# A convolution branch loaded into another tile and closed behind four projections, and the last attention head closed one pair later

## The chip, the cores and the metric

The kernel runs on one core of a Trainium2 chip. A core has five engines that run at the same time, each through its own queue of instructions in a fixed order: TensorE (PE in the profile) multiplies matrices, its weight loads are shown apart as PEld; VectorE (DVE) and ScalarE (ACT) work elementwise; GpSimd (POOL) does small elementwise work and issues DMAs; SyncE (SP) issues DMAs. An engine whose next instruction waits for a semaphore holds everything behind that instruction. The metric is the device time of one execution in microseconds (us). The kernel before took 1056.47, 1059.1 and 1056.67 us in three runs, median 1056.67.

## The reference

One layer of a streaming encoder on 512 tokens of width 1024, in float32. Four mixers are fed from one normed input and one combined projection, then gated, merged and projected:

```python
h = _rms_norm(x, norm_mix_pre[l])
(a_q, a_k, a_v, f_q, f_k, f_v, f_g, c_u, s_x, s_b, s_c) = jnp.split(h @ w_in[l], cuts, axis=-1)
ya = _diff_attention(...)                  # A: 4 heads, two score maps each, then an RMS norm per head
yf = _forgetting_attention(...)            # F: 8 heads, a cumulative log-forget bias
c_a, c_g = jnp.split(c_u + b_glu[l], 2, axis=-1)
yc = _dwconv_causal(c_a * jax.nn.sigmoid(c_g), conv_dw[l]) + conv_dw_b[l]
yc = jax.nn.silu(_layer_norm(yc, conv_ln_g[l], conv_ln_b[l]))      # C: convolution branch
ys = s_b * _dwconv_causal(s_c * s_x, sc_w[l])                      # D: short convolution
br = jnp.stack([ya, yf, yc, ys], axis=2)
proj = jnp.einsum('bsnc,ncd->bsnd', br, w_branch[l])
gates = jax.nn.sigmoid(h @ w_gate[l] + b_gate[l]).reshape(B, S, N_BRANCH, D)
mixed = jnp.sum(gates * proj, axis=2) @ w_out[l]
```

Behind the mixers come a cross-attention into 256 memory tokens and a gated MLP of width 2816. They are computed by code that the change leaves alone.

## The kernel before

Every product is made three times from split operands: a float32 value is held as a high part (a cast) and a low part (the value less its high part), and `mm3` multiplies high by high, high by low and low by high. A weight block of 128x1024 is loaded by SP into one of two `wr` tiles, cast by ACT into `wh` (line 190), and DVE makes `wl` (line 191); both have four buffers. A projection to 128 channels is 24 matmuls of 128x512 into one PSUM bank. In the stretch that matters here all projections take turns in the two banks with the tag `mm`: a projection can start only when the one two before it has been read out of its bank.

`run_blocks` walks a list of such jobs, fetches weights three jobs ahead, and after each job lets background generators (`bg`) put some of their steps into the program: the depthwise convolution and its norm (`conv_task`, `conv_norm_task`), the attention heads (`a_task`, `f_task`). A generator's `yield` says how much work the step was and how long it should wait. So the order in which instructions are written comes from this interleaving. The tile framework then sets each engine's final order with a simulated timeline; `tc.issue_after(x)` keeps an instruction behind instruction x. Tiles come from pools in rings: with `bufs=2` the third allocation of a tag takes the first one's place and waits for its last reader.

The order of jobs in the stretch: values of the A heads; queries and keys of head 0; of head 1; two gate blocks of branch C; queries and keys of head 2; four blocks of C; head 3; six blocks of C; values of the F heads; queries and keys of F pair 0; of pair 1; blocks of branch A's gate; and so on to pair 3.

What the change and the prediction touch:

- `conv_norm_task`. The convolution's result is turned to token-major through DRAM into the tile `xn`, normed, turned back through DRAM (`conv_chan`, line 720) and loaded into `xn` again by four POOL DMAs (line 724). For each of four channel blocks j, ACT then makes an Identity and a Tanh of it (lines 737, 738), DVE joins them (line 739), and `split` writes the high part on ACT (line 158) and the low part on DVE (line 159) into `y["c"]`. Blocks 0 and 1 come as soon as they can; blocks 2 and 3 wait for the keys of head 0. `xn` is in the ring `qk` with two buffers, which also holds the queries and keys of each head, so head 1's `qk` tile is `xn`'s.
- `qk_jobs`. `body_q` clears two parts of the `qk` tile on POOL (line 804) and reads the bank in two halves: ACT copies one half (line 808), DVE takes its low part (line 809), then the same for the other. `body_k` does so with two ACT copies each (lines 816, 817) and a low part (line 818). After `body_k` the dictionary `key_ends` holds the last two instructions.
- `a_task`. A head's four query tiles of 128 make scores (PE, bank tag `sc`), a masked maximum (DVE, line 882), Exp (ACT, line 887), a scaling (ACT, line 891, and DVE, line 892), transposes (PE, line 236) and products with the values. At its end the head's output goes twice through DRAM (`turn`), and line 917 on ACT scales it into the tile `z`; `split` writes it into `y["a"]`. The output tile `o` is in the ring `ck`, `z` in the ring `fbias`.
- `f_task`. The F pairs use the rings `ck` (rows of the forget bias) and `fbias` (bias tiles), and the ring `e` of three buffers that all heads use for their softmax. Pair 0 starts behind pair 1's keys.
- `mixer_jobs`. Head 3 (name `a3` in the background) is run to its end before the jobs of F pair 0.

Of the kernel before, what the change touches and what calls it, by code (L numbers as in the profile page):

```python
# [25 lines left out]
P = 128  # L26
# [57 lines left out]
def hybrid_layer(ctx: ExitStack, tc: tile.TileContext, a: dict, out: bass.AP):  # L84
# [228 lines left out]
    def e4(dtype=F32):  # L313
        return m1p.tile([P, 2, S], dtype, tag="e", name="e", bufs=3)
# [266 lines left out]
    def y8(dtype=F32R):  # L581
        return m2p.tile([P, 4, S], dtype, tag="y8", name="y8", bufs=2)

    def y8b():
        return m2bp.tile([P, 4, S], F32R, tag="y8b", name="y8b", bufs=2)

    acc = [m2p.tile([P, S], F32, tag=f"acc{m}", name=f"acc{m}") for m in range(NK)]
    y = {}
# [63 lines left out]
        yield 0.5, 0.0  # L652

    conv_ends = []
    key_ends = {}

    def conv_task(j):
        n = 31
# [29 lines left out]
        yield 0.0, 5.0  # L688

    def conv_norm_task():  # L690
        xn = m1p.tile([P, 5, S], F32, tag="qk", name="xn", bufs=2)
        tok, chan = (dram.tile([P, NT * S], F32, name=n) for n in ("conv_tok", "conv_chan"))
        yield 0.0, 2.0
        while len(conv_ends) < 4:
# [24 lines left out]
            yield 0.65, 0.0  # L719
        G.dma_start(chan, conv_y.rearrange("p j c -> p (j c)"))  # L720
        yield 0.0, 4.0
        form = chan.rearrange("(b r) (a x) -> a r b x", r=32, a=4)
        for a_ in range(4):
            G.dma_start(xn[a_ * 32:a_ * 32 + 32, :4], form[a_])
        yield 0.0, 5.0
        turned_y = xn[:, :4].rearrange("p b (j t c) -> p j t b c", j=4, t=NT)
        while "d" in y:
            yield 0.0, 2.0
        yield 0.0, 2.0
        y["c"] = (y8(), y8())  # L730
        for j in range(4):
            while j > 1 and (O_AK, 0) not in key_ends:
                yield 0.0, 0.5
            e = e4()
            one, two = (e[:, i].rearrange("p (t b c) -> p t b c", t=NT, b=4) for i in range(2))
            with tc.issue_after(key_ends[O_AK, 0][0]) if j > 1 else ExitStack():
                A.activation(one, turned_y[:, j], AF.Identity, bias=pc("ln_b", j), scale=pc("ln_g", j))
                A.activation(two, turned_y[:, j], AF.Tanh, bias=half["ln_b"][:, j:j + 1], scale=half["ln_g"][:, j:j + 1])
# [56 lines left out]
    def qk_jobs(cq, ck, j, then, tag=None):  # L795


        st = {}
        rows = (slice(0, HD), slice(HD, P))

        def body_q(hi, lo):
            qk = st["qk"] = m1p.tile([P, 6, S], F32R, tag="qk", name="qk", bufs=2)
            for c, r in enumerate(rows):
                G.memset(qk[rows[1 - c], 4 + c].bitcast(F32), 0.0)
            ps = bank(tag)
            channel_major(ps, (hi, lo), ht)
            for c, r in enumerate(rows):
                A.copy(qk[r, c], ps[r])
                V.tensor_tensor(qk[rows[1 - c], c], ps[r], qk[r, c].bitcast(F32), ALU.subtract)

        def body_k(hi, lo):
            qk = st["qk"]
            ps = bank(tag)
            channel_major(ps, (hi, lo), ht)
            for c, r in enumerate(rows):
                A.copy(qk[r, 2 + c], ps[r])
                copy = A.copy(qk[rows[1 - c], 2 + c], ps[r])
                low = V.tensor_tensor(qk[r, 4 + c], ps[r], qk[r, 2 + c].bitcast(F32), ALU.subtract)
            key_ends[ck, j] = copy.ins, low.ins
# [35 lines left out]
    def head_tile(tag):  # L855
        return m1p.tile([P, S], F32, tag=tag, name=f"head_{tag}", bufs=2)
# [3 lines left out]
    def a_task(h, qk, v):  # L860
# [56 lines left out]
        A.activation(z.rearrange("p (t b c) -> p t b c", t=NT, b=4), o.rearrange("p (b t c) -> p t b c", b=4, t=NT),  # L917
                     AF.Identity, scale=half["dn"])
        split(z, y["a"][0][:, h], y["a"][1][:, h])
        yield 0.6, 0.0  # L920

# [88 lines left out]
    def f_task(p, qk, v):  # L1010
# [6 lines left out]
            G.dma_start(t, crows[2 * p + j:2 * p + j + 1, :].rearrange("a s -> (a s)").partition_broadcast(P))  # L1017
            ck.append(t)
        yield 0.0, 2.0
        while p == 0 and (O_FK, 1) not in key_ends:  # L1020
            yield 0.0, 0.5
        es, pts, av = {}, None, None
        for step in range(6):
# [17 lines left out]
            if step < 4:  # L1041
# [3 lines left out]
                for j in range(2):  # L1045
# [9 lines left out]
                    with tc.issue_after(key_ends[O_FK, 1][1]) if p + step == 0 else ExitStack():  # L1055
# [59 lines left out]
    def then(f):  # L1115

        return None, None, f
# [4 lines left out]
    def mixer_jobs():  # L1122
# [687 lines left out]
```

## Time and profile before

| what | value |
|---|---|
| median of 3 runs | 1056.67 us (1056.47 to 1059.1) |
| the profiled execution | 1056.2 us |
| its span, first to last instruction | 1054.4 us |
| PE busy in the span | 1041.7 us, 99% |
| PEld, DVE, ACT, POOL busy | 84%, 76%, 48%, 17% |
| mean granted TensorE clock | 0.996 |
| chain of work that ended last, on PE | 96% |

The profile is one execution. Rows of its timeline give the start of an instruction from the span's start, its duration, engine, line, operation and output<-input; in square brackets stands how long the engine had been idle before it and what ended that. "x4" means four such instructions in a row, put together. Matmuls are pipelined: a row's duration reaches over the start of the next, and the distance between the starts is what a matmul takes from PE's time. So a short wait of PE is hard to see as idle time, and is read from the starts.

### The profile page before, as it was taken

The page shows a single profiled execution, that of the slowest core. Times are in us where ns is not written, and L with a number is a line of the kernel's source. Part 1 is how long each engine was busy: PE and PEld are TensorE (multiplying, and loading weights), DVE is VectorE, ACT ScalarE, POOL GpSimd, SP SyncE. Part 2 cuts the span into 40 slices and gives each one's busy share as a digit, 9 for nine tenths or more (in the row PEclk, how much of TensorE's full clock was granted, in tenths as well). Part 3 has the DMA queues.
Part 4 walks back from the last instruction along what each step waited for, and adds up shares of the span by engine and source line. Part 5 has one row for each costly group of instructions (what it writes and reads, how often), then busy time and mean ns, then how long its engine had stood idle before and what let it go on. Part 6 is the DMA issues. An engine that isn't in the chain of part 4 may idle for free.

```text
span 1054.4 us, 14556 instructions
## 1 busy us (share of the span) xinstructions
PE 1041.7 (99%) x5295; PEld 886.0 (84%) x5295; DVE 806.4 (76%) x1280; ACT 501.4 (48%) x823; POOL 182.4 (17%) x309
## 2 busy tenths in 40 slices
PE   9999999999999999999999999999999999999996
PEld 8888888888888988888888899988888888888885
DVE  6999997677767477867487798777878777777795
ACT  5322222286565374655444566554333333355571
POOL 4000000200231233433011031121112111111001
PEclk9999999999999999999999999999999999999998
DMA  8954334742342353232358644236577676626662
GB/s 262 298 165 103 102 100 141 196 112 87 105 138 83 100 161 101 80 100 82 99 167 276 216 132 129 60 104 196 186 241 231 212 234 213 198 81 211 207 191 81
DMA packets 165373, 163.08 MB, mean 155 GB/s; under 512 B 6527, under 2 KB 136172, under 8 KB 165045
## 3 DMA queue, kind: packets, MB, share of 16 engines
q1 hardware_dynamic: 152995, 119.91, 38.0%
q0 software_dynamic: 5824, 19.03, 6.0%
q10 hardware_dynamic: 6482, 23.21, 5.8%
q8 instruction: 42, 0.69, 0.3%
q14 instruction: 30, 0.25, 0.1%
HBM read 139.03 MB, written 23.09 MB: 154 GB/s over the span
## 4 chain that ended last, share of the span: by engine, by line
PE 96%; DMA 1%; DVE 1%; ACT 1%; issue 1%; POOL 1%; POOLq 0%; DVEq 0%; SPq 0%; ACTq 0%
PE ps_mm L232 51%; PE ps_av L232 30%; PE ps_sc L232 8%; PE ps_tr L232 4%; PE ps_tr L236 2%; DMA wide<-in_w_out 1%; DMA xs<-in_x 0%; POOL st_r L271 0%; DVE nt L281 0%; POOL st_m L268 0%; ACT hth L432 0%; ACT wa L412 0%; ACT wh L190 0%; DVE wl L191 0%; POOL st_m L270 0%
## 5 line engine op out<-in xcount | busy, mean ns | idle before, releaser
L190 ACT CAST wh<-wr 128x1024 fp32r<-128x1024 f32 (+1 forms) x142 | 148.8, 1049 | 262.7 <-PE ps_mm L232 165.6
L191 DVE TENSOR_TENSOR wl<-wr,wh 128x1024 fp32r<-128x1024 f32 (+1 forms) x142 | 178.2, 1256 | 72.2 <-ACT wh L190 72.0
L232 PE MATMUL ps_mm<-hth,wh 128*128 128x512 f32 (+1 forms) x592 | 221.2, 380 | 0.3 <-ACT hth L155 0.2
L232 PE MATMUL ps_mm<-htl,wh 128*128 128x512 f32 (+1 forms) x592 | 220.5, 379 | 0.2 <-DVE htl L156 0.2
L232 PE MATMUL ps_mm<-hth,wl 128*128 128x512 f32 (+1 forms) x592 | 220.4, 379 | 0.0
L232 PE MATMUL ps_av<-htl,wh 128*128 128x512 f32 (+1 forms) x352 | 131.8, 374 | 0.0
L232 PE MATMUL ps_av<-hth,wh 128*128 128x512 f32 (+1 forms) x352 | 131.8, 374 | 0.0
L232 PE MATMUL ps_av<-hth,wl 128*128 128x512 f32 (+1 forms) x352 | 131.6, 374 | 0.0
L232 PEld LDWEIGHTS ps_mm<-hth,wh 128*128 128x128 f32 x592 | 109.7, 188 | 21.1 <-ACT hth L155 0.8
L232 PEld LDWEIGHTS ps_mm<-hth,wl 128*128 128x128 f32 x592 | 109.5, 188 | 20.2
L232 PEld LDWEIGHTS ps_mm<-htl,wh 128*128 128x128 f32 x592 | 109.5, 188 | 20.0 <-DVE htl L156 0.4
L665 DVE SCALAR_TENSOR_TENSOR y<-y,par,y 128x482 f32<-128x482 f32 (+29 forms) x120 | 83.3, 735 | 0.1
L232 PEld LDWEIGHTS ps_av<-hth,wl 128*128 128x128 f32 x352 | 66.2, 188 | 11.7
L232 PEld LDWEIGHTS ps_av<-htl,wh 128*128 128x128 f32 x352 | 66.1, 188 | 11.8
L232 PEld LDWEIGHTS ps_av<-hth,wh 128*128 128x128 f32 x352 | 66.1, 188 | 11.8
L1603 DVE TENSOR_TENSOR wl<-dw,wh 128x1024 fp32r<-128x1024 f32 x32 | 40.1, 1262 | 12.9 <-ACT wh L1602 12.7
L1602 ACT CAST wh<-dw 128x1024 fp32r<-128x1024 f32 x32 | 33.5, 1052 | 23.1 <-PE ps_mm L232 7.4
L1049 POOL TENSOR_SCALAR fbias<-ck,cq 128x128 f32<-128x128 f32 (+3 forms) x32 | 27.7, 872 | 63.6 <-DVE st L1056 57.2
L1551 ACT ACTIVATE th<-c 128x512 f32<-128x512 f32 x22 | 13.9, 632 | 47.7 <-DVE c L594 47.7
L155 ACT CAST pth<-ps_tr 128x512 fp32r<-128x512 f32 (+3 forms) x56 | 23.6, 449 | 26.2 <-PE ps_tr L236 25.9
L594 DVE SCALAR_TENSOR_TENSOR c<-ps_mm,par,c 128x510 f32<-128x510 f32 (+1 forms) x44 | 32.7, 744 | 0.7
L156 DVE TENSOR_TENSOR ptl<-ps_tr,pth 128x512 fp32r<-128x512 f32 (+3 forms) x56 | 27.5, 512 | 7.2 <-ACT pth L155 7.1
(491 smaller groups left out, 2130.6 us busy)
## 6 DMA issues: line engine op xcount, KB each, us to landing
wr<-in_w_up SPq DMA_DIRECT2D x44, 512.0 KB
wr<-in_w_in SPq DMA_DIRECT2D x38, 512.0 KB
wr<-in_w_gate SPq DMA_DIRECT2D x32, 512.0 KB
wp<-in_w_down ACTq DMA_DIRECT2D x22, 512.0 KB
sums<-wp ACTq DMA_DIRECT2D x22, 512.0 KB
dw<-sums SPq DMA_DIRECT2D x44, 256.0 KB
wr<-in_w_branch SPq DMA_DIRECT2D x16, 512.0 KB
wide<-in_w_out SPq DMA_DIRECT2D x12, 512.0 KB
```

Of the source, the lines that this page charges most:

```text
L155: A.copy(hi, ps)
L156: V.tensor_tensor(lo, ps, hi.bitcast(F32), ALU.subtract)
L190: order(A.copy(hi, raw[:, :n]))
L191: low.tensor_tensor(lo, raw[:, :n], hi.bitcast(F32), ALU.subtract)
L232: PE.matmul(ps, lhs, rhs, start=start, stop=stop)
L236: PE.transpose(ps, x, ident[:n, :n])
L594: ins = V.scalar_tensor_tensor(dst[:, s:], src[:, :S - s], w(k), dst[:, s:], ALU.mult, ALU.add)
L665: ins = V.scalar_tensor_tensor(dst[:, s:], src[:, :S - s], pc("conv_dw", k * 4 + j), dst[:, s:], ALU.mult, ALU.add)
L1049: G.tensor_scalar(bias[:, :w], ck[j][:, :w], -1.0, cq[:, qt, head:head + 1], ALU.mult, ALU.add)
L1551: A.activation(th, c[:, 0], AF.Tanh, scale=0.5)
L1602: A.copy(hi, x)
L1603: V.tensor_tensor(lo, x, hi.bitcast(F32), ALU.subtract)
```

## The change

The convolution branch's channel-major data no longer goes back into `xn`. It is loaded into a tile of the ring `y8b`, which holds the branch D operand before and the branch A operand later and is free in between; the load waits in the program until the D operand is dropped. `xn` itself stays in the ring `qk` for the token-major part only. Its four channel blocks are put behind four projections in turn: block 0 behind head 0's queries, 1 behind its keys, 2 behind head 1's queries, 3 behind its keys. `qk_ends` takes the place of `key_ends` and records queries too.

For head 3 the output tile and `z` are the two halves of one tile of the ring `e`, where they were in `ck` and `fbias`. The head is run up to the issue of its last DMAs before F pair 0's jobs; the closing activation and the split come behind the keys of F pair 1, and F pair 0 starts behind them.

```diff
-    def y8b():
-        return m2bp.tile([P, 4, S], F32R, tag="y8b", name="y8b", bufs=2)
+    def y8b(dtype=F32R):
+        return m2bp.tile([P, 4, S], dtype, tag="y8b", name="y8b", bufs=2)
...
     def conv_norm_task():
-        xn = m1p.tile([P, 5, S], F32, tag="qk", name="xn", bufs=2)
+        xn = m1p.tile([P, 6, S], F32, tag="qk", name="xn", bufs=2)
...
         G.dma_start(chan, conv_y.rearrange("p j c -> p (j c)"))
         yield 0.0, 4.0
+        while "d" in y:
+            yield 0.0, 2.0
+        xn = y8b(F32)
         form = chan.rearrange("(b r) (a x) -> a r b x", r=32, a=4)
         for a_ in range(4):
-            G.dma_start(xn[a_ * 32:a_ * 32 + 32, :4], form[a_])
+            G.dma_start(xn[a_ * 32:a_ * 32 + 32], form[a_])
...
         for j in range(4):
-            while j > 1 and (O_AK, 0) not in key_ends:
+            after = ((O_AQ, 0), (O_AK, 0), (O_AQ, 1), (O_AK, 1))[j]
+            while after not in qk_ends:
                 yield 0.0, 0.5
             e = e4()
...
-            with tc.issue_after(key_ends[O_AK, 0][0]) if j > 1 else ExitStack():
+            with tc.issue_after(qk_ends[after][0]):
...
-        o = head_tile("ck")
+        last = e4() if h == 3 else None
+        o = last[:, 0] if h == 3 else head_tile("ck")
         sq = head_tile("fbias")
         yield from turn(o, x, NT, sq, f"head_chan{h}", True)
+        heads_at[h] = "turned"
+        while h == 3 and (O_FK, 1) not in qk_ends:
+            yield 0.0, 0.5
...
-        z = head_tile("fbias")
-        A.activation(z.rearrange("p (t b c) -> p t b c", t=NT, b=4), o.rearrange("p (b t c) -> p t b c", b=4, t=NT),
-                     AF.Identity, scale=half["dn"])
+        z = last[:, 1] if h == 3 else head_tile("fbias")
+        with tc.issue_after(qk_ends[O_FK, 1][0]) if h == 3 else ExitStack():
+            A.activation(z.rearrange("p (t b c) -> p t b c", t=NT, b=4), o.rearrange("p (b t c) -> p t b c", b=4, t=NT),
+                         AF.Identity, scale=half["dn"])
+        heads_at[h] = "done"
         split(z, y["a"][0][:, h], y["a"][1][:, h])
...
-        while p == 0 and (O_FK, 1) not in key_ends:
+        while p == 0 and ((O_FK, 1) not in qk_ends or heads_at[3] != "done"):
...
-        yield then(lambda: bg.drain("a3"))
+        yield then(lambda: bg.drain("a3", lambda: heads_at[3] == "turned"))
         yield from kv_blocks(0)
         ga = gate_blocks(0, "a")
         for p in range(1, 4):
             yield from kv_blocks(p)
+            yield then(lambda: bg.drain("a3"))
```

What this does to the order of instructions is shown at three places, the first of them on two engines. The line numbers of the changed kernel are two to nine higher (808 becomes 810, 816 and 817 become 819 and 820, 737 and 738 become 739 and 740, 887 becomes 890, 917 becomes 925).

ACT, from the keys of head 0 to the second half of head 1's queries; before:

```order
L737 ACTIVATE e<-xn,par_403 128x512
L738 ACTIVATE e<-xn,s_ln_b,s_ln_g 128x512
L190 CAST wh<-wr 128x1024
L737 ACTIVATE e<-xn,par_403 128x512
L738 ACTIVATE e<-xn,s_ln_b,s_ln_g 128x512
L158 ACTIVATE y_1748<-e 128x512
L808 CAST qk<-ps_mm 64x512
L887 ACTIVATE e,st_1919<-e,st_1919 128x128 x2
L158 ACTIVATE y_1748<-e 128x512
L808 CAST qk<-ps_mm 64x512
```

The same place now, and on to the first copies of head 1's keys:

```order
L739 ACTIVATE e<-y8b,par_403 128x512
L740 ACTIVATE e<-y8b,s_ln_b,s_ln_g 128x512
L190 CAST wh<-wr 128x1024
L810 CAST qk<-ps_mm 64x512
L158 ACTIVATE y_1785<-e 128x512
L890 ACTIVATE e,st_1914<-e,st_1914 128x128 x2
L810 CAST qk<-ps_mm 64x512
L739 ACTIVATE e<-y8b,par_403 128x512
L740 ACTIVATE e<-y8b,s_ln_b,s_ln_g 128x512
L894 ACTIVATE e<-e,st_1914 128x128
L190 CAST wh<-wr 128x1024
L819 CAST qk<-ps_mm 64x512
```

One channel block (an Identity, a Tanh and a high part) has moved from ahead of the two copies of head 1's queries to behind them, and the first copy stands directly behind the weight cast.

PE, the second gate block of branch C behind head 1, with the transposes of head 0's second query tile (`ps_tr`) and the first scores of head 1 (`ps_sc`); before:

```order
L232 MATMUL ps_mm<-hth,wh 128x512
L236 MATMUL ps_tr<-ident,e 128x128 x2
L232 MATMUL ps_sc<-qk 128x128 x2
L232 MATMUL ps_mm<-htl,wh 128x512
L232 MATMUL ps_sc<-qk 128x128 x2
L232 MATMUL ps_mm<-hth,wl 128x512
L232 MATMUL ps_mm<-hth,wh 128x512
```

And now:

```order
L232 MATMUL ps_sc<-qk 128x128 x2
L232 MATMUL ps_mm<-hth,wh 128x512
L232 MATMUL ps_sc<-qk 128x128 x2
L232 MATMUL ps_mm<-htl,wh 128x512
L232 MATMUL ps_mm<-hth,wl 128x512
L232 MATMUL ps_mm<-hth,wh 128x512
L236 MATMUL ps_tr<-ident,e 128x128 x2
L232 MATMUL ps_mm<-htl,wh 128x512
```

The transposes, which had 16 matmuls of this block ahead of them, have 22 now and stand behind head 1's scores.

ACT, the copies of F pair 1's queries and keys and the close of head 3 (`head_fbias<-head_ck,s_dn` is `z<-o`); before:

```order
L808 CAST qk<-ps_mm 64x512
L917 ACTIVATE head_fbias<-head_ck,s_dn 128x512
L155 CAST y8b<-head_fbias 128x512
L808 CAST qk<-ps_mm 64x512
L190 CAST wh<-wr 128x1024
L816 CAST qk<-ps_mm 64x512
L817 CAST qk<-ps_mm 64x512
L816 CAST qk<-ps_mm 64x512
L817 CAST qk<-ps_mm 64x512
L1061 ACT_TABLE_LOAD
L1061 ACTIVATE e,st_3568<-e,st_3568 128x128 x2
```

And now:

```order
L810 CAST qk<-ps_mm 64x512 x2
L190 CAST wh<-wr 128x1024
L819 CAST qk<-ps_mm 64x512
L820 CAST qk<-ps_mm 64x512
L819 CAST qk<-ps_mm 64x512
L820 CAST qk<-ps_mm 64x512
L925 ACTIVATE e<-e,s_dn 128x512
L155 CAST y8b<-e 128x512
L1070 ACT_TABLE_LOAD
L1070 ACTIVATE e,st_3568<-e,st_3568 128x128 x2
L190 CAST wh<-wr 128x1024
```

The closing activation and its split have left the place between the two query copies and stand ahead of F pair 0's first Exp.

POOL, the end of the convolution's norm (the MEMSETs clear the `qk` tiles of heads 1 to 3); before:

```order
L268 TENSOR_TENSOR st_m<-bn_1564,nhalf 128x1
L271 TENSOR_TENSOR st_r<-st_m,nhalf 128x1
L720 DMA conv_chan<-y_385 128x2048
L724 DMA xn<-conv_chan 32x4x512 x4
L804 MEMSET qk 64x512 x6
```

And now:

```order
L268 TENSOR_TENSOR st_m<-bn_1564,nhalf 128x1
L271 TENSOR_TENSOR st_r<-st_m,nhalf 128x1
L720 DMA conv_chan<-y_385 128x2048
L806 MEMSET qk 64x512 x2
L727 DMA y8b<-conv_chan 32x4x512 x4
L806 MEMSET qk 64x512 x4
```

The clearing of head 1's tile stands ahead of the four loads instead of behind them. SP's order is unchanged, and from the end of F pair 1's keys on so is PE's.

More of the change, by code (lines that the diff above doesn't have):

```diff
@@ L654, in hybrid_layer @@
     conv_ends = []
-    key_ends = {}
+    qk_ends = {}
     def conv_task(j):
@@ L721, in conv_norm_task @@
         yield 0.0, 4.0
+        while "d" in y:
+            yield 0.0, 2.0
+        xn = y8b(F32)
         form = chan.rearrange("(b r) (a x) -> a r b x", r=32, a=4)
         for a_ in range(4):
[L724 removed]
+            G.dma_start(xn[a_ * 32:a_ * 32 + 32], form[a_])
         yield 0.0, 5.0
[L726 to L728 removed]
+        turned_y = xn.rearrange("p b (j t c) -> p j t b c", j=4, t=NT)
         yield 0.0, 2.0
@@ L807, in body_q @@
             for c, r in enumerate(rows):
-                A.copy(qk[r, c], ps[r])
-                V.tensor_tensor(qk[rows[1 - c], c], ps[r], qk[r, c].bitcast(F32), ALU.subtract)
+                copy = A.copy(qk[r, c], ps[r])
+                low = V.tensor_tensor(qk[rows[1 - c], c], ps[r], qk[r, c].bitcast(F32), ALU.subtract)
+            qk_ends[cq, j] = copy.ins, low.ins
         def body_k(hi, lo):
@@ L818, in body_k @@
                 low = V.tensor_tensor(qk[r, 4 + c], ps[r], qk[r, 2 + c].bitcast(F32), ALU.subtract)
-            key_ends[ck, j] = copy.ins, low.ins
+            qk_ends[ck, j] = copy.ins, low.ins
             then(qk)
@@ L1054, in f_task @@
                     scores(ps, qk, j, qt * P, w)
-                    with tc.issue_after(key_ends[O_FK, 1][1]) if p + step == 0 else ExitStack():
+                    with tc.issue_after(qk_ends[O_FK, 1][1]) if p + step == 0 else ExitStack():
                         V.tensor_tensor_reduce(e[:, j, :w], ps[:, :w], bias[:, :w], scale=1.0,
```

## The prediction

> **What bounds the kernel.** I read the page's busy times and chain first, then the stretches of the program side by side, then, because that shows no idle PE, the starts of single instructions.
>
> ```profile
> PE 1041.7 (99%) x5295; PEld 886.0 (84%) x5295; DVE 806.4 (76%) x1280; ACT 501.4 (48%) x823; POOL 182.4 (17%) x309
> 33.20:204.40 171.20, 171.20 (x769) 142.22 (x768) 154.80 (x226) 46.47 (x55) 9.42 (x20) 1.00 0.52 153
> 209.70:395.00 185.30, 185.25 (x985) 158.94 (x985) 123.71 (x273) 113.29 (x216) 37.76 (x70) 1.00 0.39 113
> 215.36 10.88 PE ps_mm L232 x48
> ```
>
> The first row is the page. The next two are stretches in us with their length, then the busy time of PE, PEld, DVE, ACT and POOL: first the part ahead of the attention, then the part that the change reorders. The last is a piece of the chain: 48 matmuls in 10.88 us, 0.227 us each. PE is busy for 185.25 of the 185.30 us that the change touches, and its total work stays the same. So the change can win only waits hidden in the distances between matmuls, and lose whatever new wait it makes.
>
> Two such waits stand out. Both are at the first gate block behind a pair of projections, and both have the two `mm` banks as cause. Here are PE's starts at head 1 and at F pair 1; at the undisturbed scores of head 0 for comparison; and the DVE instruction that reads the bank for the last time.
>
> ```profile
> 226.08 0.56 PE L232 MATMUL ps_sc<-qk 128*128 128x128 f32 x4
> 226.47 0.45 PE L232 MATMUL ps_mm<-hth,wh 128*128 128x512 f32 x1
> ...
> 232.23 0.40 PE L232 MATMUL ps_mm<-hth,wl 128*128 128x512 f32 x1
> 232.65 0.47 PE L232 MATMUL ps_mm<-hth,wh 128*128 128x512 f32 x1
> ...
> 388.10 0.56 PE L232 MATMUL ps_sc<-qk 128*128 128x128 f32 x4
> 388.68 0.47 PE L232 MATMUL ps_mm<-hth,wh 128*128 128x512 f32 x1
> ```
>
> ```profile
> 231.81 0.69 DVE L809 TENSOR_TENSOR qk<-ps_mm,qk 64x512 fp32r<-64x512 f32 x1
> ...
> 387.84 0.69 DVE L809 TENSOR_TENSOR qk<-ps_mm,qk 64x512 fp32r<-64x512 f32 x1
> ```
>
> From 232.23 to 232.65 are 0.42 us where 0.23 is usual: 0.19 us of wait. From 388.10 to 388.68 are 0.58 where the same four scores took 0.39 at 226.08: 0.19 again. The low parts of the query bank end at 231.81 + 0.69 = 232.50 and 387.84 + 0.69 = 388.53, and both times the gate block starts 0.15 us later. So what ends last there is the reading of a query bank.
>
> **Part one: the convolution blocks.** Why is head 1's query bank read late?
>
> ```profile
> 225.46 0.81 ACT L738 ACTIVATE e<-xn,s_ln_b,s_ln_g 128x512 f32<-128x512 f32 x1
> 226.17 1.04 ACT L190 CAST wh<-wr 128x1024 fp32r<-128x1024 f32 x1
> 227.10 0.82 ACT L737 ACTIVATE e<-xn,par 128x512 f32<-128x512 f32 x1
> 227.82 0.81 ACT L738 ACTIVATE e<-xn,s_ln_b,s_ln_g 128x512 f32<-128x512 f32 x1
> 228.53 0.62 ACT L158 ACTIVATE y<-e 128x512 fp32r<-128x512 f32 x1
> 229.17 0.58 ACT L808 CAST qk<-ps_mm 64x512 fp32r<-64x512 f32 x1
> 229.65 0.40 ACT L887 ACTIVATE e<-e,st 128x128 f32<-128x128 f32 x1
> ...
> 230.44 0.62 ACT L158 ACTIVATE y<-e 128x512 fp32r<-128x512 f32 x1
> 231.08 0.58 ACT L808 CAST qk<-ps_mm 64x512 fp32r<-64x512 f32 x1
> ```
>
> ```profile
> 228.74 1.10 POOL L804 MEMSET qk<- 64x512 f32 x2 [21.58 <-ACT e L738]
> ```
>
> ```profile
> 228.59 0.16 DVE L885 TENSOR_SCALAR st<-st 128x2 f32<-128x2 f32 x1
> ```
>
> Head 1's `qk` tile is `xn`'s (the POOL row waits 21.58 us for the last Tanh), so its copies stand behind block 3. With `xn` elsewhere the first copy can stand directly behind the cast, at 227.1 instead of 229.17. The first Exp needs the DVE row at 228.59 + 0.16 = 228.75; in ACT's new order it has only block 1's high part ahead of it and goes at 228.8 instead of 229.65. Two Exps at 0.40 each bring the second copy to 229.7 (was 231.08), done 230.3. On DVE the low part of block 1 (0.69), the two small softmax steps (0.4) and the low part of the query come behind 229.4: the bank is free at about 231.1 instead of 232.50. PE wants it at 232.46. The 0.19 us go, with 1.2 us to spare.
>
> What is late next: gate block 2 wants the bank of head 1's keys.
>
> ```profile
> 235.97 0.58 ACT L816 CAST qk<-ps_mm 64x512 fp32r<-64x512 f32 x1
> 236.56 0.58 ACT L817 CAST qk<-ps_mm 64x512 fp32r<-64x512 f32 x1
> ...
> 237.18 0.69 DVE L818 TENSOR_TENSOR qk<-ps_mm,qk 64x512 fp32r<-64x512 f32 x1 [0.79 <-ACT qk L817]
> ...
> 239.04 0.39 PE L232 MATMUL ps_mm<-hth,wh 128*128 128x512 f32 x1
> ```
>
> Before, the bank is free at 237.87 and wanted at 239.04 - 0.15 = 238.89: 1.0 us to spare. Now block 2's high part (0.62) stands among the key copies, against one short wait that it partly fills; the second copies end at about 237.4 and the low part at 238.1. Wanted, with PE 0.19 earlier, at 238.7: 0.6 to spare. I take 0, the value nearest to these rows. Bounds: 0, and 0.8 if the two other pieces of a block (2 x 0.72, by the starts at 227.10 and 227.82) came in front as well, 1.44 - 0.6.
>
> Blocks 2 and 3 (each 0.72 + 0.71 + 0.62 = 2.05 us of ACT) now stand among head 0's Exps and scalings.
>
> ```profile
> 237.90 0.48 DVE L892 SCALAR_TENSOR_TENSOR e<-e,st 128x256 f32<-128x256 f32 x1
> ```
>
> ```profile
> 242.67 0.38 PE L236 MATMUL ps_tr<-ident,e 128*128 128x128 f32 x2
> ```
>
> The second query tile was scaled at 237.90 + 0.48 = 238.4 and transposed at 242.67: 4.3 us of cover. One block more in front makes it 2.05 later, about 2.5 with the small waits between; in PE's new order the transposes also stand six matmuls (1.4 us) further back. So 4.3 + 1.4 - 2.5 = 3.2 us of cover stay, and later steps catch up, since ACT is busy for only 113.29 of the 185.30 us. Cost 0; bounds 0 and the 4.1 us of both blocks.
>
> The other edits of this part cost nothing, for these reasons:
>
> ```profile
> 204.96 2.19 POOL L724 DMA_DIRECT2D xn<-conv_chan  x4 [4.92 <-DMA conv_chan<-y]
> ```
>
> ```profile
> 212.94 0.81 ACT L737 ACTIVATE e<-xn,par 128x512 f32<-128x512 f32 x1 [1.45 <-DMA xn<-conv_chan]
> ```
>
> The four loads come 1.1 us later, since the MEMSETs of head 1 (1.10 at 228.74) stand ahead of them on POOL's queue; these wait for nothing, as `conv_chan` was sent after `xn`'s last reader. So the data lands at about 212.9 + 1.1 = 214.0. Its first reader, block 0, now stands behind head 0's query copies, after 217; before, ACT sat 1.45 us idle for it. Behind POOL's loads nothing is due until head 2's MEMSETs. SP's queue is as it was.
>
> **Part two: head 3's close.**
>
> ```profile
> 383.22 0.57 ACT L808 CAST qk<-ps_mm 64x512 fp32r<-64x512 f32 x1
> 385.71 0.72 ACT L917 ACTIVATE head_fbias<-head_ck,s_dn 128x512 f32<-128x512 f32 x1 [1.92 <-DMA head_ck<-head_chan]
> 386.46 0.62 ACT L155 CAST y8b<-head_fbias 128x512 fp32r<-128x512 f32 x1
> 387.11 0.58 ACT L808 CAST qk<-ps_mm 64x512 fp32r<-64x512 f32 x1
> ...
> 392.26 1.28 ACT L1061 ACT_TABLE_LOAD   x1
> ...
> 394.34 0.39 ACT L1061 ACTIVATE e<-e,st 128x128 f32<-128x128 f32 x1
> ```
>
> ```profile
> 384.88 0.68 DVE L809 TENSOR_TENSOR qk<-ps_mm,qk 64x512 fp32r<-64x512 f32 x1
> ```
>
> ```profile
> 399.27 0.38 PE L236 MATMUL ps_tr<-ident,e 128*128 128x128 f32 x2
> ...
> 400.42 0.62 PE L232 MATMUL ps_mm<-y8b,wh 128*128 128x512 f32 x2
> ```
>
> ACT waits 1.92 us for a DMA in front of the second query copy, and the close takes another 0.72 + 0.62. Without them that copy needs only the first low part, done at 385.56; it ends at 386.2, its low part at 386.9 instead of 388.53, and PE wants the bank at 388.5. The second 0.19 us go. The close moves behind the key copies, to 392.3, 6 us after its data. It puts 1.34 us in front of the table load and the first Exps of F pair 0, whose transposes PE runs at 399.27: the last of these Exps ended at 394.73, so of 4.5 us of cover, DVE's scaling in it, 3.2 remain. The low part of `y["a"]` comes at about 394.4 and is first used at 400.42. F pair 0 is held only until the close is in the program, which is the same round of the background as before. The tile of the ring `e` is idle there, as no softmax runs between head 3 and pair 0. All at 0.
>
> **The sum.** The profiled execution took 1056.2, 1.8 more than its span. 1056.2 - 0.19 - 0.19 = 1055.8. The median of the runs is 0.47 above the profiled execution, so I forecast 1056.67 - 0.38 = 1056.3 for the median. That is 0.04%, and counts as no change: 0.3% (3.2 us) is about what a measurement of this kernel can tell from none.
>
> One row might speak for far more to win: in the touched stretch the weight loads are busy for only 158.94 of 185.30 us, 86%. If the other 14% were waits of PE, 26 us would be hidden there. Against it, the stretch without attention, where nothing interrupts the projections, has 142.22 of 171.20, 83%: the share is that of an undisturbed pitch of 0.227 us. The Trainium skill (Perfetto Trace Analysis, Identifying the Most-Contended Engine) has the rule behind this: matmul busy time does not tell how near PE is to its limit, and the busy share of the weight loads is to be taken instead. By that rule alone the kernel would have room down to about 1030, where the rows give 1056.3; the trace does not bear it out here, since the share is no higher where nothing waits.
>
> **Rivals.**
> - The win comes back elsewhere: the bank of gate block 2 (up to 0.8 us), or a few of PE's transposes and value products, newly placed, wait some tenths each. For it: the two waits of 0.19 show that PE is scheduled to within tenths of its data. Against: the spare times above. Time: 1056.3 to 1058.
> - Slower: ACT's new load in front of head 0. If head 0's chain from Exp to transposes is late by more than its cover (3.2 us beyond what I allow, the point from which it decides), PE stands at the transposes, and as PE runs in order the projections stand with it; each of the two blocks then shows in full. 1056.3 + 4.1 = 1060.4. For it: ACT's rows from 225.46 to 229.65 stand without any idle time. Against: PE's order moved back with it.
> - The change doesn't do what it says: another instruction holds the two banks. Against it is the 0.15 us between bank reading and gate block, twice the same. Time 1056.7.
> - Faster by far: the 14% that the weight loads leave free are waits after all, and the freed banks take an eighth of the 26 us: 1053.4. Against it stands the 83%.
>
> **Chances.** Forecast 0.52; win comes back 0.26; no effect 0.06; slower by ACT's load or a like pile-up 0.13; far faster 0.03. Faster by over 0.3%: 0.03; within: 0.52 + 0.26 + 0.06 = 0.84; slower: 0.13. The range takes in the first three cases: below, the forecast less twice the 0.47 between profiled execution and median, 1055.3; above, 1058.2, the first rival's end with a little for the runs.
>
> **What would show it.** Right: the starts of PE at the first gate block of head 1 and of F pair 1 lie 0.23 and 0.39 apart from what stands ahead; the low part of head 1's queries ends over 1 us before that; ACT has no wait for `head_chan` between the two query copies of pair 1; the stretch up to F pair 1's keys is 0.4 us shorter, all later ones equal. Wrong: a distance of over 0.5 us between PE's starts in front of a transpose of head 0 or of gate block 2; ACT waiting for the loads of `y8b`.

## The result, and the profile after

Both kernels were timed 17 times:

| kernel | median | lowest to highest | runs above 1057.4 us |
|---|---|---|---|
| before | 1057.57 us | 1056.06 to 1061.68 | 9 of 17 |
| changed | 1055.79 us | 1055.22 to 1057.36 | 0 of 17 |

The ratio is 0.9979, with a 95% interval of 0.9970 to 0.9988: 1.8 us less in the median, inside the 0.3% that counts as no change. The forecast time of 1056.3 is met within about 0.5 us, and that is in part luck. The forecast was a gain of 0.38 us, from two waits of 0.19; the measured gain is 1.8. It started from a median of 1056.67 of three runs, where the 17 have 1057.57; from there 0.38 less would be 1057.2. What it lacks is something of 1 to 5 us that the kernel before has in about half of its runs, and that the first profile doesn't contain. The mark of 1057.4 us was set behind the result, just above the changed kernel's longest run; executions above it are called long here.

The profiled execution took 1055.79 us, its span 1054.0 (before: 1056.2 and 1054.4). Counted from the same matmul at 209 us, PE is 0.40 us earlier than before at 395 us. 0.17 of it is there at 364 us, behind the first place; the rest comes at F pair 1. These are the two places, now without a wait. Behind 690 us the lead varies between 0.27 and 0.69 us, at places that vary between profiles of the kernel before as well. First the stretch (times as before: PE, PEld, DVE, ACT, POOL), then ACT, DVE and PE at head 1:

```profile
209.70:395.00 185.30, 185.30 (x987) 159.15 (x986) 123.32 (x272) 112.43 (x211) 38.07 (x68) 1.00 0.40 113
```

```profile
227.60 0.58 ACT L810 CAST qk<-ps_mm 64x512 fp32r<-64x512 f32 x1
...
229.15 0.40 ACT L890 ACTIVATE e<-e,st 128x128 f32<-128x128 f32 x1 [0.44 <-DVE st L888]
...
230.06 0.58 ACT L810 CAST qk<-ps_mm 64x512 fp32r<-64x512 f32 x1
```

```profile
230.91 0.69 DVE L811 TENSOR_TENSOR qk<-ps_mm,qk 64x512 fp32r<-64x512 f32 x1
...
237.63 0.69 DVE L821 TENSOR_TENSOR qk<-ps_mm,qk 64x512 fp32r<-64x512 f32 x1 [0.90 <-ACT qk L820]
```

```profile
232.09 0.40 PE L232 MATMUL ps_mm<-hth,wl 128*128 128x512 f32 x1
232.33 0.39 PE L232 MATMUL ps_mm<-hth,wh 128*128 128x512 f32 x1
...
238.59 0.39 PE L232 MATMUL ps_mm<-hth,wh 128*128 128x512 f32 x1
...
387.81 0.56 PE L232 MATMUL ps_sc<-qk 128*128 128x128 f32 x4
388.20 0.44 PE L232 MATMUL ps_mm<-hth,wh 128*128 128x512 f32 x1
```

PE's starts at head 1 lie 0.24 apart (before 0.42), at F pair 1 0.39 (before 0.58). Head 1's query bank is free at 231.60, 0.73 us ahead of the gate block's start at 232.33: taking off the 0.15 us from a bank's reading to PE's start, 0.6 us to spare. The bank of gate block 2 is free at 238.32, and used at 238.59: in the same way, 0.12 us to spare.

At F pair 1, ACT no longer waits for a DMA between the query copies, only for DVE; the close comes behind the key copies:

```profile
382.79 0.57 ACT L810 CAST qk<-ps_mm 64x512 fp32r<-64x512 f32 x1
385.17 0.58 ACT L810 CAST qk<-ps_mm 64x512 fp32r<-64x512 f32 x1 [1.81 <-DVE qk L811]
...
391.90 0.72 ACT L925 ACTIVATE e<-e,s_dn 128x512 f32<-128x512 f32 x1
```

What is left to explain is the gain of 1.8 us in the runs where the two profiles differ by 0.4, and why the changed kernel's runs no longer scatter.

### The profile page after: what moved, and what is told of

The parts are those of the page before. It is cut to its first block, busy times and chain, and to the rows that moved or that the text cites. A ratio compares the mean times of both kernels' runs of the same rounds, so it can differ in the third digit from the quotient of the medians.

```text
span 1054.0 us, 14559 instructions
## 1 busy us (share of the span) xinstructions
PE 1041.7 (99%) x5295; PEld 886.8 (84%) x5295; DVE 807.1 (77%) x1280; ACT 501.9 (48%) x823; POOL 184.3 (17%) x309
## 4 chain that ended last, share of the span: by engine, by line
PE 99%; DVE 0%; ACT 0%; issue 0%; POOL 0%; POOLq 0%; DVEq 0%; ACTq 0%
PE ps_mm L232 51%; PE ps_av L232 31%; PE ps_sc L232 8%; PE ps_tr L232 4%; PE ps_tr L236 2%; PE ps_mm L442 1%; PE ps_av L442 1%; PE ps_mm L384 0%; PE ps_sc L389 0%; DVE o L1710 0%; PE ps_tr L426 0%; POOL st_m L270 0%; POOLq L1816 0%; ACT hth L155 0%; ACT hth L432 0%
```

## Experiments

**The two halves of the change.** `conv_only` is the changed kernel with head 3 closed as before; `head3_only` is the kernel before with head 3's close alone moved.

```diff
 conv_only, against the changed kernel
-        last = e4() if h == 3 else None
-        o = last[:, 0] if h == 3 else head_tile("ck")
+        o = head_tile("ck")
...
-        z = last[:, 1] if h == 3 else head_tile("fbias")
-        with tc.issue_after(qk_ends[O_FK, 1][0]) if h == 3 else ExitStack():
+        z = head_tile("fbias")
...
-        yield then(lambda: bg.drain("a3", lambda: heads_at[3] == "turned"))
+        yield then(lambda: bg.drain("a3"))
```

> Only part one of the change (the convolution's data in the y8b tile, one channel block behind each of four projections); head 3 is closed as before. Fixed waits (the forecast's theory): 0.19 us less than the kernel before, the wait of PE at the first gate block of head 1 gone, the one at F pair 1 still there; the spread of its times as wide as that of the kernel before (some 5 us). Late landings at the convolution (the load of conv_chan stands in ACT's queue ahead of head 0's query copies, and comes late in some executions): 1.5 us or more less in the median, and a spread of some 2 us, as the changed kernel has. Late landings at head 3 (the load of head_chan between two query copies of F pair 1): 0.2 us less, spread as before.

> Only part two (head 3's close behind F pair 1's keys, its tile in the softmax ring); the convolution as before. Fixed waits: 0.19 us less than the kernel before, the wait at F pair 1 gone, the one at head 1 still there, spread of the times as before. Late landings at the convolution: 0.2 us less, spread as before (some 5 us). Late landings at head 3: 1.5 us or more less in the median and a spread of some 2 us.

The experiments were run in four sessions, on three chips, each with the kernel before timed beside them; its own share of long executions there is 7 of 23, 6 of 23, 10 of 13 and 10 of 17, so a variant is compared only with the runs beside it.

Measured, with 23 runs of the kernel before beside them (median 1056.59, up to 1062.2, 7 above 1057.4): `conv_only` 1058.52 median (1057.21 to 1059.85, 11 runs), ratio 1.0011 [0.9998, 1.0024]; `head3_only` 1056.23 (1055.44 to 1061.8, 12 runs, 4 above 1057.4), ratio 1.0001 [0.9986, 1.0015].

`head3_only` is as both the fixed waits and the late landing at the convolution have it: in its trace the stretch from 209 to 395 us is 0.18 us shorter, and the scatter stays. `conv_only` is as no theory had it: by the medians 1.9 us slower. The interval of its ratio just reaches no change, but 10 of its 11 runs are long, and its lowest is 2.0 us above the changed kernel's lowest. The profiled execution is its longest, 1059.85. Its ACT rows at F pair 1, its PE rows, and two windows (time, PE's busy time and its matmuls, ...; the last three numbers are the granted clock, the DMA share, GB/s):

```profile
384.81 0.73 ACT L920 ACTIVATE head_fbias<-head_ck,s_dn 128x512 f32<-128x512 f32 x1 [3.14 <-DMA head_ck<-head_chan]
385.44 1.03 ACT L190 CAST wh<-wr 128x1024 fp32r<-128x1024 f32 x1
386.38 0.57 ACT L810 CAST qk<-ps_mm 64x512 fp32r<-64x512 f32 x1
...
388.48 0.58 ACT L810 CAST qk<-ps_mm 64x512 fp32r<-64x512 f32 x1 [1.00 <-DVE qk L811]
```

```profile
387.53 0.56 PE L232 MATMUL ps_sc<-qk 128*128 128x128 f32 x4
390.04 0.67 PE L232 MATMUL ps_mm<-hth,wh 128*128 128x512 f32 x1 [1.96 <-DVE qk L811]
390.51 0.63 PE L232 MATMUL ps_mm<-htl,wh 128*128 128x512 f32 x1
```

```profile
390.04:393.45 3.41, 3.41 (x8) 2.69 (x9) 2.12 (x4) 2.60 (x6) 2.35 (x4) 0.51 0.70 185
394.00:396.00 2.00, 2.00 (x10) 1.67 (x9) 1.01 (x6) 1.43 (x5) 1.43 (x4) 1.00 0.26 76
```

The scheduler has put head 3's close ahead of both query copies and the weight cast, where it was between the copies. ACT waits 3.14 us for the load there, both copies are late, and PE stands 2.51 - 0.39 = 2.12 us. Then eight matmuls run at a granted clock of 0.51, 0.43 us apart in place of 0.23: 1.6 us more. In this execution a stand of 2.1 us has cost 3.7. So the halves can't be added: part one alone turns head 3's wait from 0.19 us into one of 2.1, or 3.7 with the half clock, and part two takes that away again. For the scatter, `conv_only` is inside its expectation for a late landing at the convolution: 2.6 us from lowest to highest, with a constant loss on top.

**The kernel before, profiled again.**

> The kernel before, unchanged, for one more profiled execution. If late landings make its times scatter, the execution profiled here is longer than 1056.2 us by what PE's starts show as one or a few large distances, behind a row of ACT that waits for the load of conv_chan or of head_chan. If the scatter has another source, PE's starts around the two places are those of the first profile to 0.1 us, whatever the time is.

> As before_look_1: one more profiled execution of the unchanged kernel. Late landings: where the execution is longer than 1056.2 us, the surplus lies at PE's starts behind ACT's wait for conv_chan or head_chan. Another source: it lies elsewhere, or is spread over the whole span.

> The kernel before, unchanged, once more profiled. In a slow execution (over 1057.4 us), by the theory: ACT's wait for conv_chan is longer than the 1.45 us of the first profile, PE stands at head 0's first scores, and the granted clock is low for some us behind it. Otherwise as the looks before.

> The kernel before, unchanged, once more profiled. In a slow execution (over 1057.4 us), by the theory: the last packet of the conv_chan loads later than in the looks before, PE stands at head 0's first scores, perhaps with half a clock behind it. In one below, none of that. Rival: a slow execution without a stand of PE there.

> The kernel before, unchanged, once more profiled, as in the look ahead of it: by the theory a slow execution shows a stand of PE at head 0's first scores behind a late landing; by the rival it shows none there.

They took 1055.81, 1056.59, 1057.37, 1055.62 and 1056.74 us; none is one of the long executions. PE never stands in front of head 0's first scores; the 0.42 to 0.45 us at head 1 is in all of them (0.42 in the first profile). What they do show is where other scatter comes from: up to 1.4 us between executions lies ahead of 33 us, and in the third and the fifth 0.55 and 0.40 us more between 690 and 760 us, both far from the change.

**The landing made late on purpose.** `before_late` and `after_late` put four small DMAs ahead of the four loads on POOL; `before_late_2` puts two.

```diff
+        junk = m1p.tile([P, 64], F32, tag="junk", name="junk", bufs=1)
+        late = [G.dma_start(junk[a_ * 32:a_ * 32 + 32], form[a_, :, 0, :64]) for a_ in range(4)]
         for a_ in range(4):
-            G.dma_start(xn[a_ * 32:a_ * 32 + 32, :4], form[a_])
+            with tc.issue_after(late[-1].ins):
+                G.dma_start(xn[a_ * 32:a_ * 32 + 32, :4], form[a_])
```

> The kernel before, with four small DMAs more on POOL's queue in front of the four loads of conv_chan (each reads 32x64 of conv_chan into a tile that nobody reads), so that the loads go out and land some 2.2 us later (4 x 0.55, the price of a load in the profile's POOL row). Late landing at the convolution is what costs the kernel before its slow executions: PE stands 1.2 to 1.9 us at head 0's first scores (the delay less 0.35 us to spare at 226.08 and less a high part that ACT now writes behind the first copy), and a stand of that size brings the half clock seen in conv_only, 1.6 us more: 2.8 to 3.5 us longer in the profiled execution, and in the median of the runs. Rival (ACT's wait there is covered): below 0.5 us.

> The changed kernel with the same four small DMAs in front of its four loads of conv_chan. Late landing: nothing, within 0.3 us of the changed kernel's 1055.8, since the first reader (block 0, behind head 0's query copies) comes several us behind the landing. Rival (the change has only moved the wait): 1 us or more, with ACT waiting for the loads in front of block 0.

> As before_late, with two of the small DMAs in place of four: the loads of conv_chan go out some 1.1 us later. On ACT one high part of the convolution (0.62 us) now stands behind the first query copy in place of ahead of it; the rest of ACT's order, at head 3 too, is that of the kernel before. Late landing at the convolution as the source of the slow executions: PE stands 0.2 to 1.0 us at head 0's first scores (1.1 less up to 0.6 for the high part, less 0.35 to spare, plus the landing's own scatter), so the median is 0.3 to 2 us above that of the kernel before, and more than half of the runs are above 1057.4, since the half clock comes with some of the stands. Rival (that wait is covered, slow executions come from elsewhere): median within 0.3 us, and the share of slow executions as before, about a third.

| kernel | median (lowest to highest, runs) | kernel before, beside it | PE's loss at head 0's first scores |
|---|---|---|---|
| `before_late` | 1062.23 (1061.6 to 1063.93, 4) | 1056.66 | 3.74 us |
| `after_late` | 1056.47 (1055.78 to 1057.06, 10) | 1056.66 | none |
| `before_late_2` | 1060.65 (1058.22 to 1062.1, 10) | 1058.69 | 3.02 us |

The loss is that of PE's later matmuls against the first profile, counted from 209 us to 229 us. The late landing makes every run of the two variants of the kernel before long. For `before_late` that is clear (ratio 1.0051 [1.0031, 1.0072]). For `before_late_2` it is clear in the trace alone: its median is 2 us higher, but the kernel before beside it has 10 of 13 long runs, and the ratio, 1.0009 [0.9988, 1.0029], doesn't tell the two apart. In the changed kernel the landing costs nothing between 209 and 395 us, where PE's starts gain the same 0.40 us. Its median is 0.7 above that kernel's 1055.79, where 0.3 was expected, but the changed kernel wasn't timed beside it, and 0.63 us of the difference of the two profiles lie ahead of 209 us. The first reader of the loads follows the query copies without a wait:

```profile
218.71 0.58 ACT L813 CAST qk<-ps_av 64x512 fp32r<-64x512 f32 x1 [1.52 <-DVE qk L814]
219.32 0.82 ACT L742 ACTIVATE e<-y8b,par 128x512 f32<-128x512 f32 x1
```

The sizes were expected too small. In `before_late` PE stands 2.1 us and then runs at half the clock, as in `conv_only` (rows below). Behind 231 us the scheduler has changed PE's order too, so the rest of this run's time isn't the landing's alone: of its other 2.1 us, 1.4 are lost at F pair 1, where the close stands ahead of both query copies again.

```profile
228.23 0.62 PE L232 MATMUL ps_mm<-hth,wh 128*128 128x512 f32 x1
228.65 0.63 PE L232 MATMUL ps_mm<-htl,wh 128*128 128x512 f32 x1
```

And `before_late_2`, whose loads go out only 0.7 to 1.0 us later against PE than in the profiles of the kernel before, made ACT wait 5.73 us, longer than the 5.03 of `before_late`. Its rows of POOL, SP and ACT:

```profile
205.18 2.21 POOL L727 DMA_DIRECT2D xn<-conv_chan  x4
```

```profile
206.42 0.37 SPq L176 DMA_DIRECT2D wr<-in_w_gate  x1
```

```profile
216.79 0.82 ACT L740 ACTIVATE e<-xn,par 128x512 f32<-128x512 f32 x1 [5.73 <-DMA xn<-conv_chan]
```

So the time at which the loads go out isn't all. The row of SP gives the clue: the next weight block (512 KB) goes out while POOL issues its four loads (1 MB), and the profile has both on the same 16 DMA engines.

**One part undone.** `after_front` puts blocks 0 and 1 back in front of head 0's query copies on ACT, and leaves all else in the program as changed; the order that the scheduler makes of it differs on PE only behind 231 us.

```diff
-            after = ((O_AQ, 0), (O_AK, 0), (O_AQ, 1), (O_AK, 1))[j]
-            while after not in qk_ends:
+            after = (None, None, (O_AQ, 1), (O_AK, 1))[j]
+            while after and after not in qk_ends:
...
-            with tc.issue_after(qk_ends[after][0]):
+            with tc.issue_after(qk_ends[after][0]) if after else ExitStack():
```

> The changed kernel with one part undone: channel blocks 0 and 1 of the convolution stand again in front of head 0's query copies on ACT, as before; tile, loads, blocks 2 and 3, and head 3 as changed. Late landing at the convolution, by ACT's place: the profiled execution within 0.3 us of the changed kernel's 1055.8, but the slow executions come back: about a third of the runs above 1057.4, and a spread of 4 us or more. Rival (the tail is removed by the other tile, or by blocks 2 and 3): no more than one run above 1057.4, as the changed kernel has it (0 of 17).

Measured: 1057.31 median (1055.75 to 1060.59), 6 of 12 runs above 1057.4; ratio to the kernel before 1.001 [0.9997, 1.0022]. The long executions are back, and its profiled execution (1057.48 us, where 1055.8 within 0.3 was expected) is one. ACT's first row for the convolution, and PE at head 0's first scores:

```profile
215.52 0.82 ACT L739 ACTIVATE e<-y8b,par 128x512 f32<-128x512 f32 x1 [4.38 <-DMA y8b<-conv_chan]
```

```profile
225.72 0.22 PE L232 MATMUL ps_sc<-qk 128*128 128x128 f32 x1
226.30 0.30 PE L232 MATMUL ps_sc<-qk 128*128 128x128 f32 x1 [0.36 <-DVE qk L821]
227.41 0.33 PE L232 MATMUL ps_sc<-qk 128*128 128x128 f32 x1 [0.82 <-ACT qk L820]
228.24 0.30 PE L232 MATMUL ps_sc<-qk 128*128 128x128 f32 x1 [0.49 <-DVE qk L821]
228.37 0.45 PE L232 MATMUL ps_mm<-hth,wh 128*128 128x512 f32 x1
```

ACT waits 4.38 us in place of 1.45, and its lateness goes through head 0's copies to PE, which stands 2.65 - 0.39 = 2.26 us. No DMA was added here. It has the changed kernel's loads, and lands as late as that kernel; only the place of two blocks on ACT makes the lateness count. From the records of the DMA packets (POOL's last issue of the four loads against SP's issue of the weight block, and the start of the loads' last data packet behind that last issue, us):

```
kernel                        last load - weight block   last packet
before (six profiles), head3_only -0.66 to -0.25          4.9 to 5.4
conv_only                             -0.14                  7.5
after_front                            0.04                  7.7
changed                                0.24                  7.5
before_late_2                          0.42                  8.6
after_late                             1.51                  7.2
before_late                            2.56                  5.7
```

In these traces, where POOL has issued all four loads at least 0.25 us ahead of SP's weight block, they land first. Where it is 0.14 us ahead or later, the two share the engines: in the changed kernel the loads' rate falls from about 130 KB to 8 to 60 KB in half a microsecond while the weight block passes. Then they land about 2 to 3.7 us later. No kernel has traces on both sides, so the tile and the dummies differ along with the order; what speaks for the order is the fall of the rate while the weight block passes. (In `before_late` the weight block is so far ahead that it is through before most of the loads.)

**The close race undone.** The kernel before, with two of the four loads on SP's queue, where they stand ahead of the weight block by themselves. The first two channel blocks are pinned behind the same weight cast as before, so that the order on PE, ACT and DVE stays the same instruction by instruction (the two traces have it so).

```diff
         for a_ in range(4):
-            G.dma_start(xn[a_ * 32:a_ * 32 + 32, :4], form[a_])
+            (G if a_ < 2 else SP).dma_start(xn[a_ * 32:a_ * 32 + 32, :4], form[a_])
...
+        held = [wh_casts[n_casts + 3 - 1].ins]
...
-            with tc.issue_after(key_ends[O_AK, 0][0]) if j > 1 else ExitStack():
+            with tc.issue_after(key_ends[O_AK, 0][0] if j > 1 else held[-1]):
```

> The kernel before, with two of the four loads of conv_chan issued by SP in place of POOL; every other instruction of PE, ACT and DVE stands where it stood. In the ten traces without dummies the loads land 4.9 to 5.4 us behind POOL's last issue where that issue is at least 0.25 us ahead of SP's issue of the next weight block, and 7.5 to 7.7 us behind it where it is 0.14 us ahead or later: the weight block then shares the DMA engines with the loads. Theory (the slow executions of the kernel before are those that lose this race, which POOL's 4 x 0.55 us of issuing makes close): with two loads on each queue POOL's last issue lies some 1.3 us ahead of the weight block, SP's two stand ahead of it in its own queue, so the slow executions are gone: at most one run in ten above 1057.4, median 1055.8 to 1056.8, the wait of 0.19 us at head 1's gate block still there. Rival (the landing is late for another reason, or the slow executions come from elsewhere): a third or more of the runs above 1057.4, as in the runs of the kernel before beside it.

Measured: 1056.22 median (1055.62 to 1057.27), none of 12 runs above 1057.4; the kernel before beside it 1057.64 (1056.16 to 1061.45), 10 of 17 above. Ratio 0.9983 [0.9972, 0.9994]: 1.4 us. Its rows of POOL, SP and ACT:

```profile
205.31 1.11 POOL L726 DMA_DIRECT2D xn<-conv_chan  x2 [4.97 <-DMA conv_chan<-y]
```

```profile
205.11 0.83 SPq L726 DMA_DIRECT2D xn<-conv_chan  x2
207.12 0.39 SPq L176 DMA_DIRECT2D wr<-in_w_gate  x1
```

```profile
212.46 0.81 ACT L743 ACTIVATE e<-xn,par 128x512 f32<-128x512 f32 x1 [0.69 <-issue]
```

POOL's last issue stands 1.24 us ahead of the weight block, ACT waits 0.69 us, and PE runs through head 0's scores; the 0.43 us at head 1 are still there. So the long executions of the kernel before go when these four loads can't be passed, and by the medians 1.4 of the 1.8 us that the change brings in the runs can be had without it. The 0.4 us of the two fixed waits make up the rest, though not more exactly than the intervals allow (0.6 to 3.0 us for the 1.4, 1.3 to 3.2 for the 1.8).

One link is inferred. No profiled execution of the unchanged kernel was a long one, so the lost race is seen in `after_front` and `before_late_2`, not in that kernel itself. `before_split` also lands 0.3 to 0.8 us earlier against PE than the profiled executions of the kernel before; that alone would not cover a landing 2 us late.

## Why the prediction was right, and where it was not

- **The two hidden waits.** Right in place, cause and size: 0.38 us forecast, 0.40 in the profile after. The rival by which another instruction holds the banks has fallen with it.
- **Part one's times on ACT.** The first query copy at 227.60 (forecast 227.1), the first Exp at 229.15 (228.8), the bank free at 231.60 (231.1): half a microsecond late (the Exp 0.35), since the weight cast ahead of them starts at 226.54 where it was 226.17. The cover was larger, but the sign that the low part of head 1's queries ends over 1 us ahead of the gate block wasn't met: it is 0.73. At gate block 2 the 0.6 us to spare were 0.12: the rival by which the win comes back there missed by a tenth of a microsecond.
- **The four loads.** This is the step that failed, twice. "The four loads come 1.1 us later, since the MEMSETs of head 1 stand ahead of them": the MEMSETs ran in POOL's wait for `conv_chan` and cost the loads nothing there. Yet against PE the last load goes out 0.5 us later: the first follows the landing of `conv_chan` by 0.53 us (before 0.29), and 0.23 us lie between the first and the others. (Its row names a matmul as what ended the wait, but in all three traces with such a row the distance to that landing is 0.53 to 0.54.) Why isn't settled, but it takes the last load from 0.25 us ahead of the weight block to 0.24 behind it (rows below). "The data lands at about 214.0": the last packet came at 214.45, and ACT could have used it about 1.3 us later (that distance in `after_front`), for another reason than the one given, the weight block. Both errors were covered, by the place behind the query copies.

```profile
205.06 0.57 POOL L727 DMA_DIRECT2D y8b<-conv_chan  x1 [3.96 <-PE ps_mm L232]
205.86 1.64 POOL L727 DMA_DIRECT2D y8b<-conv_chan  x3 [0.23 <-issue]
```

```profile
206.71 0.37 SPq L176 DMA_DIRECT2D wr<-in_w_gate  x1
```

- **The 1.45 us of ACT's wait.** The prediction read them, in one profile, as idle time that costs nothing and goes away. They were the sign of a queue whose head hangs on a DMA, with little margin behind it: in `after_front` ACT starts 2.9 us later against PE than in the first profile, and 2.26 of that reach PE. A DMA still stands at that place in the changed kernel: ACT waits there 4.55 us for the weight block itself, but the first query copy comes 0.77 us earlier against PE than before (rows below). The forecast's only scatter was the 0.47 us between the profiled execution and the median of three runs, and one of those three, 1059.1, was already a long execution. The term left out of the sum is this kernel's share of long executions: 1.4 us in the median of the runs here.

```profile
215.91 1.05 ACT L190 CAST wh<-wr 128x1024 fp32r<-128x1024 f32 x1 [4.55 <-DMA wr<-in_w_gate]
216.86 0.57 ACT L810 CAST qk<-ps_av 64x512 fp32r<-64x512 f32 x1
```

- **Part two.** The queue hazard was the same (1.92 us for `head_chan`), but it didn't scatter: `head3_only` has the tail of the kernel before. What the prediction didn't see is that with part one alone, the scheduler would have made this a stand of 2.1 us, or 3.7 with the half clock; the two parts were costed as if each stood alone.
- **Slower by ACT's load.** Did not come: no distance in front of a transpose, and head 0's chain stayed inside its cover. **Faster by far.** Did not come either: the weight loads are busy for 159.15 of 185.30 us, 86% as before, with the waits gone. So the share says nothing about room here.

## What to carry to other kernels

Where an in-order engine waits for a DMA in front of work that the bound engine needs, count the margin behind that wait, even if the profile shows the bound engine at 99%: the profile is one draw of the landing. Look which other transfer goes out within a microsecond of it; here who went first was worth 2 to 3.7 us of landing, and moving the consumer behind the work that must not wait removed the long executions as well as winning the race did. Read the spread of the runs as part of the profile: three runs with one 2.4 us above the others were the evidence.

## What was not expected of the hardware

A stand of PE of 2.1 us was followed by eight matmuls at half the granted clock (0.51 in the window shown of `conv_only`, 0.50 in `before_late`), 1.6 us more. Stands of 2.26 us in `after_front` and 3.0 us, in four pieces, in `before_late_2` were not:

```profile
228.60:231.60 3.00, 3.00 (x14) 2.45 (x14) 2.67 (x8) 1.81 (x7) 0.00 (x0) 1.00 0.11 21
```

(`after_front`, the 3 us behind its stand: clock 1.00, 14 matmuls.) So the size of a stand alone doesn't decide. The record of the granted clock in the traces shows what does. From its first rise on, every stretch at one clock inside the span, up to the last fall at its end, is a whole multiple of 3.41 us: 113 of them ahead of the half clock in `conv_only` and 65 in `before_late`, one at the half clock in both, and 305 or 306 in the twelve traces without one. If the span is cut at these multiples, PE's idle time in a single piece (its length less PE's busy time there) puts the cases in order:

| run | piece, us | PE idle in it | clock in the next piece |
|---|---|---|---|
| `conv_only` | 386.72 to 390.14 | 1.96 | 0.50 |
| `before_late`, head 0 | 224.93 to 228.35 | 1.55 | 0.50 |
| `before_late`, F pair 1 | 392.19 to 395.60 | 1.46 | 1.00 |
| `before_late_2` | 224.31 to 227.73 | 1.30 | 1.00 |
| `after_front` | 226.94 to 230.35 | 0.97 | 1.00 |

The larger stands of `after_front` and `before_late_2` lie across a cut (226.94 and 227.73), so neither piece has enough. The first rise comes at 4.3 to 7.5 us of the span, at another time in each trace, so where a stand falls among the cuts differs from execution to execution. These are five cases, and PE's busy time is modelled, so the border between 1.46 and 1.55 us is known from them alone. The Trainium skill (TensorE: Matmul & The Clock Gate, What's actually happening) has a free-running window of about 3.4 us, and the pieces of 3.41 us agree; that 1.55 us of idle time in a piece suffice differs from its full idle window, and here the measurement decides. The long runs of the kernel before agree: a mean granted clock of 0.994 to 0.996 in those above 1061 us, 0.996 to 0.998 in those below 1057.4; one piece at half clock would take 0.0016 off the mean.

How two transfers pass in the DMA engines was not settled: the order was decided by 0.1 to 0.4 us of issue time, and no run here varied this alone in fine steps.
